# A hybrid decoder layer on one core: key norms and values by transposes, sums and centring on VectorE, and a new written-out order

## The chip, the core and the metric

The kernel runs on one core of a Trainium2 chip, and the times are microseconds on the device. The core has TensorE (PE in the profile, with its weight loads as PEld), VectorE (DVE), ScalarE (ACT), GpSimd (POOL) and SyncE (SP), which here only issues transfers. What counts is the median over several runs of the whole program.

## What is computed

One decoder layer on 512 tokens with 16 meta tokens ahead of them, model width 1024, 16 heads of 64. A first layer norm feeds one projection `h @ w_in`, whose columns are queries, keys and values of a sliding-window attention, the inputs of an RWKV-7 time mixing, and two gates. The two branches are gated and added, then follow an output projection, a layer norm, a squared-ReLU MLP of width 4096 and a last layer norm. The change is in the RWKV branch. Cut to what matters (per head, `N` = 64 channels):

```
kk = kh * k_k
kk = kk / max(sqrt(sum(kk * kk)), 1e-12)                      # the key norm
S  = S * w + (S @ -kk) (kk * a)^T + v k^T                     # 64 x 64 state, per token
y  = S @ r
y  = (y - mean(y)) * rsqrt(mean((y - mean(y))^2) + eps) * lnx_g + lnx_b
y  = (y + sum(r * kh * r_k) * v) * g
```

## The kernel before

**The RWKV branch.** The heads are taken in 8 pairs (`rwkv(j)`, from line 904; two heads fill the 128 partitions), and the 512 tokens in 8 chunks of 64. Channels lie on partitions and tokens along the rows at first. For each pair the projections of key, receptance and value come from `dense` (line 621): the weights are split into a high and a low part, and each product is three matmuls (`three`, line 453, whose lines 454, 455 and 456 are the three). The recurrence is turned into matrix work: scores between the tokens of a chunk (`scores`, 1028), an inverse of each chunk's triangular matrix (its 32 x 32 blocks by substitution on GpSimd, 1119 to 1127; put back together by `inv3` and `inv4` on TensorE, 1143 to 1157), two folding steps (`fold_w`, `fold_g`), and then a chain of 8 links over the chunks: a matmul (`link`, 1243) whose halves are scaled into the next state by VectorE (1225) and ScalarE (1228). `outs` (1248) makes the outputs Y.

**The three places that the change touches.**

- `norms` (984): for each block of 128 tokens one fp32 matmul with the squared keys `sq` as weights and a constant of two columns, `ones2`, as the moving operand. The sums over the 64 channels of each head come out with tokens on partitions, ten columns in all (lines 987 and 988). One more small product (989) writes to the same PSUM tile. VectorE clips (992) and inverts (994) the ten columns, and GpSimd spreads them (999, 1008) to where they scale NT (1039) and others.
- `turn_v` (1093) and `meta0` (1193): the values are turned, so that tokens come to lie on partitions, by fp32 matmuls with a constant `center` = identity minus 1/64 within a head. So the values that enter the recurrence have their mean over the head's channels taken out already, and with them Y: the group norm after it needs no mean.
- the norm of Y (1258 to 1277): ScalarE squares Y out of PSUM (1264), VectorE sums over the 64 channels (1265), scales and adds eps (1266), GpSimd raises to the power -1/2 (1267), VectorE multiplies Y, again out of PSUM, into `yn` (1268), TensorE turns it (1273), ScalarE applies gain and bias (1276). The last pair does this in two halves.

A `pe.transpose` is a matmul with the identity that goes through in one instruction. An fp32 `pe.matmul` shows in the profile as two matmul instructions (x64 for 32 calls).

**What sets the order of the work.** Everything from the first layer norm to the start of the MLP is recorded as operations of a plan (3087 of them; one may issue several instructions), numbered as the program text makes them. The list `ORDER` says in which order they are issued, and `SLOTS` which buffer of its ring each new tile takes: `Plan.order` (354) plays the two lists and asserts that they respect the dependencies. The cost in each `op(...)` is not used by the program. Each engine executes its own operations in that order, and waits where an input is not there. The tiles of PSUM are one ring of 8 banks (`rg`, 491). The MLP behind it (from line 1543) has its own schedule by due times and isn't touched.

Of the kernel before, what the change touches and what calls it, by code (L numbers as in the profile page):

```python
# [14 lines left out]
AF = mybir.ActivationFunctionType  # L15
# [61 lines left out]
for _name, _c in ROWS:  # L77
# [304 lines left out]
def hybrid_layer_kernel(ctx: ExitStack, tc: tile.TileContext, I: dict, out: bass.AP):  # L382
# [26 lines left out]
    def cv(name):  # L409
        a, w = CONSTS[name]  # L410
        return con[:, a : a + w]
# [1621 lines left out]
```

## Time and profile before

| | |
|---|---|
| median of 3 runs | 897.17 us (896.9 to 897.31) |
| the profiled execution, its own time | 897.01 us |
| its span, first to last instruction | 895.2 us |
| mean granted TensorE clock | 0.994 of full speed |
| HBM | 107.56 MB read, 8.21 MB written, 129 GB/s over the span |

Busy times, from the page's first part, are those in which an engine has an instruction in work. The matmuls are pipelined, so that one of 290 ns may start 120 ns after the one before it: what a group of them costs is read from the starts in the timeline. In a view by stretches each row gives a stretch, its length, the busy time and the number of instructions of each engine, the granted clock of TensorE (1.00 is full speed) and the transfers' share. In the waits each row has who waited, for whom, the sum, the count and the longest.

The plan's part ends at about 575 us; the MLP fills the rest.

### The profile page before, as it was taken

What the parts mean: (1) busy time and instruction counts of PE and PEld (TensorE: products, weight loads), DVE (VectorE), ACT (ScalarE), POOL (GpSimd) and SP (SyncE); (2) the same over time, 40 slices, a digit from 0 to 9 for tenths busy, and PEclk for the clock granted to TensorE, in tenths of its full rate; (3) what the DMA queues carried; (4) which work ended last, traced back from release to release, by engine and by line L of the source; (5) the groups of instructions that cost most, each with busy time, mean ns of one, the idle gap of its engine ahead of it and who ended that gap; (6) DMA issues with size and microseconds to landing.
All of it is one profiled execution on the core that took longest, in us unless ns stands there. A gap on an engine that the chain in (4) does not pass through costs nothing.

```text
span 895.2 us, 17524 instructions
## 1 busy us (share of the span) xinstructions
PE 874.7 (98%) x6712; PEld 768.1 (86%) x6712; DVE 674.4 (75%) x1192; ACT 518.8 (58%) x1131; POOL 263.2 (29%) x672
## 2 busy tenths in 40 slices
PE   7999999999999999999989999999999999999996
PEld 6999989888898998887878877988898989888885
DVE  6882976868868678478497689598877896788757
ACT  7854568466575494483663745765556655564710
POOL 3138164183461721822816502000010000000001
PEclk9999999999999999999989999999999999999999
DMA  7443323424143242223243631395687578576322
GB/s 272 127 130 104 86 75 107 117 64 131 55 123 101 78 109 85 84 70 101 72 109 102 197 102 59 97 299 132 178 209 216 141 202 256 133 209 165 98 91 94
DMA packets 73533, 115.87 MB, mean 129 GB/s; under 512 B 40311, under 2 KB 47737, under 8 KB 69481
## 3 DMA queue, kind: packets, MB, share of 16 engines
q1 hardware_dynamic: 69728, 98.89, 35.5%
q0 software_dynamic: 2880, 14.68, 9.0%
q8 instruction: 53, 0.87, 0.4%
q10 hardware_dynamic: 840, 1.17, 0.4%
q14 instruction: 32, 0.25, 0.1%
HBM read 107.56 MB, written 8.21 MB: 129 GB/s over the span
## 4 chain that ended last, share of the span: by engine, by line
PE 90%; DVE 8%; issue 1%; ACT 1%; DMA 1%; POOL 0%; DVEq 0%; SPq 0%; ACTq 0%
PE g L454 12%; PE g L455 11%; PE g L456 11%; PE dnR L1798 7%; PE rq L1704 5%; PE tp L1704 4%; PE dnP L1798 4%; PE last L1798 4%; PE dnT L1798 3%; PE up L454 3%; PE up L455 3%; PE up L456 3%; PE g L1243 2%; PE g L1182 2%; PE g L1297 2%; PE g L1031 1%
## 5 line engine op out<-in xcount | busy, mean ns | idle before, releaser
L454 PE MATMUL g<-hhi,whi 128*128 128x512 f32 (+3 forms) x640 | 213.1, 333 | 0.2 <-DVE GR L1045 0.2
L455 PE MATMUL g<-hlo,whi 128*128 128x512 f32 (+3 forms) x640 | 204.0, 319 | 1.6 <-DVE hlo L817 1.6
L456 PE MATMUL g<-hhi,wlo 128*128 128x512 f32 (+3 forms) x640 | 203.6, 318 | 0.0
L454 PEld LDWEIGHTS g<-hhi,whi 128*128 128x128 f32 x640 | 121.0, 189 | 12.6 <-issue 2.2
L455 PEld LDWEIGHTS g<-hlo,whi 128*128 128x128 f32 x640 | 121.2, 189 | 9.6 <-DVE hlo L817 2.1
L456 PEld LDWEIGHTS g<-hhi,wlo 128*128 128x128 f32 x640 | 120.9, 189 | 8.5 <-DVE wlo L613 0.2
L613 DVE TENSOR_TENSOR wlo<-wraw,whi 128x512 fp32r<-128x512 f32 x126 | 88.3, 708 | 30.4 <-ACT whi L611 29.9
L1122 POOL TENSOR_TENSOR ftmp<-Xf,Nf 108x84 f32<-108x84 f32 (+23 forms) x248 | 86.8, 350 | 74.9 <-DMA Nf<-Nd 45.9
L611 ACT CAST whi<-wraw 128x512 fp32r<-128x512 f32 x126 | 77.0, 619 | 54.0 <-PE g L455 24.6
L1126 POOL TENSOR_TENSOR Xf<-Xf,ftmp 108x84 f32<-108x84 f32 (+23 forms) x248 | 89.6, 361 | 19.0
L1788 POOL DMA_DIRECT2D braw<-in_w_ff_dram x12 | 10.7, 890 | 206.1 <-DVE wlo L1605 87.2
L1228 ACT ACTIVATE Z<-g,PC 64x64 f32<-64x64 f32 x64 | 19.7, 308 | 65.2 <-DVE Z L1225 39.9
L1267 POOL TENSOR_TENSOR rs<-rs,mhalf 128x8 f32<-128x8 f32 (+1 forms) x9 | 14.9, 1659 | 76.2 <-DVE rs L1266 76.2
L1605 DVE TENSOR_TENSOR wlo<-wraw,whi 128x1024 fp32r<-128x1024 f32 x22 | 26.9, 1222 | 13.2 <-ACT whi L1601 10.6
L1225 DVE TENSOR_SCALAR Z<-g,PC 64x64 f32<-64x64 f32 x64 | 17.6, 274 | 23.3 <-PE g L1243 20.8
L1601 ACT CAST whi<-wraw 128x1024 fp32r<-128x1024 f32 x22 | 22.9, 1042 | 17.5 <-PE dnR L1798 8.7
L1605 DVE TENSOR_TENSOR wlo<-braw,whi 128x1024 fp32r<-128x1024 f32 x25 | 30.5, 1219 | 2.4 <-ACT whi L1601 2.4
L1605 DVE TENSOR_TENSOR blo<-braw,bhi 128x1024 fp32r<-128x1024 f32 x25 | 30.5, 1219 | 1.6 <-ACT bhi L1601 1.5
L1601 ACT CAST whi<-braw 128x1024 fp32r<-128x1024 f32 x25 | 26.3, 1053 | 5.4 <-PE rq L1704 4.6
L656 DVE SCALAR_TENSOR_TENSOR res<-g,vc,res 128x256 f32<-128x256 f32 (+2 forms) x34 | 16.2, 481 | 17.0 <-ACT res L653 16.8
L1601 ACT CAST bhi<-braw 128x1024 fp32r<-128x1024 f32 x25 | 26.3, 1051 | 3.4 <-DMA braw<-in_w_ff_dram 3.4
L454 PE MATMUL up<-h1hi,whi 128*128 128x512 f32 x72 | 28.1, 390 | 0.0
(532 smaller groups left out, 2469.6 us busy)
## 6 DMA issues: line engine op xcount, KB each, us to landing
wraw<-in_w_in_dram SPq DMA_DIRECT2D x52, 512.0 KB
braw<-in_w_ff_dram SPq DMA_DIRECT2D x19, 1024.0 KB
wraw<-in_w_ff_dram SPq DMA_DIRECT2D x32, 512.0 KB
braw<-in_w_ff_dram POOLq DMA_DIRECT2D x12, 1024.0 KB, 8.8
wraw<-in_w_out_dram SPq DMA_DIRECT2D x14, 256.0 KB
Nf<-Nd SPq DMA_DIRECT2D x24, 144.0 KB
res<-in_x_dram SPq DMA_DIRECT2D x4, 512.0 KB
G<-in_consts_dram SPq DMA_DIRECT2D x16, 128.0 KB
```

The lines of the kernel that those rows point to most:

```text
L454: pe.matmul(ps, whi, xhi, start=first, stop=False)
L455: pe.matmul(ps, whi, xlo, start=False, stop=False)
L456: pe.matmul(ps, wlo, xhi, start=False, stop=last)
L611: AC(512, lambda hi=hi, qs=qs: act.copy(hi.t, raw.t[:, qs]), plain=True, r=[raw], w=[hi], new=[hi])
L613: f = lambda hi=hi, lo=lo, qs=qs, e=e: e.tensor_tensor(lo.t, raw.t[:, qs], hi.t.bitcast(F32), op=ALU.subtract)
L1122: sub(nj * nt, lambda s=s, nj=nj, nt=nt, tv=tv: pool.tensor_tensor(tv(), Xf.t[:, 0:nj, s : s + 1].to_broadcast([NB, nj, nt]), Nf.t[:, s : ...
L1126: sub(nj * nt, lambda s=s, nj=nj, tv=tv: pool.tensor_tensor(Xf.t[:, 0:nj, s + 1 :], Xf.t[:, 0:nj, s + 1 :], tv(), op=ALU.add), port=1, r=[ ...
L1228: op("ACT", 335, lambda: act.activation(Z.t[H2[1], c, 1, :], src(1), AF.Copy, scale=PC.t[H2[1], last : last + 1]), r=[ps, PC], w=[(Z, ("s" ...
L1601: act.copy(like(s["r"][0][:, :n], s["x"]), s["x"])
L1605: dve.tensor_tensor(lo, s["x"], hi.bitcast(F32), op=ALU.subtract)
L1704: pe.matmul(o, l[:, ks], r[:, k], start=start and k == c == 0, stop=stop and k == 3 and c == 2, skip_group_check=True)
L1798: pe.matmul(acc[b], l[:, as_], r[:, ws], start=first and i == 0 and q == 0, stop=last and i == NP - 1 and q == 2, skip_group_check=True)
```

## The change

It does four things. (1) `norms` turns the squared keys by transposes into a PSUM tile of its own (`kt_`; the first 128 tokens once more into `mt`, for the meta tokens), and VectorE sums each row's 64 channels into `d1`. (2) `turn_v` and `meta0` turn the values by transposes, without centring. (3) So Y has a mean: VectorE sums it over the channels into a new small tile `ym`, and subtracts it (`yn` = Y - mean); the square and the last multiplication take `yn` from SBUF in place of Y from PSUM. (4) The constants `center` and `ones2` (130 columns) go, and `ORDER` and `SLOTS` are replaced by others, over 3105 operations. The words given with the change say that the order was searched with shared PSUM tiles, transfer semaphores and the clock counted.

```diff
-    out["center"] = np.eye(P) - bones / HD
-    out["ones2"] = (p[:, None] // HD) == np.arange(2)[None, :]
...
+    rym = ring("ym", rb, [P, 8], 2)
...
-        mt, d1, dv, dvm = Buf(rg), Buf(rd1), new("dv", rdv), Buf(rdvm)
+        mt, kt_, d1, dv, dvm = Buf(rg), Buf(rg), Buf(rd1), new("dv", rdv), Buf(rdvm)
...
-                pe.matmul(mt.t[:, 2 * i : 2 * i + 2], sq.t[:, t0 : t0 + P], cv("ones2"), start=True, stop=True)
-            pe.matmul(mt.t[:, 8:10], sq.t[:, 0:P], cv("ones2"), start=True, stop=True)
+                pe.transpose(kt_.t[:, i * P : (i + 1) * P], sq.t[:, t0 : t0 + P], ident)
+            pe.transpose(mt.t[:, P : 2 * P], sq.t[:, 0:P], ident)
             pe.matmul(mt.t[0:48, 32:64], BKm.t, AXm.t.rearrange("p e t -> p (e t)"), start=True, stop=True)
 
-        op("PE", 1300, norms, r=[sq, BKm, AXm], w=[(mt, "s")], new=[mt], mode="F")
-        op("DVE", 80, lambda: dve.tensor_scalar(d1.t, mt.t[:, 0:10], 1e-24, None, op0=ALU.max), r=[(mt, "s")], w=[d1], new=[d1])
-
-        op("DVE", 120, lambda: dve.reciprocal(d1.t, d1.t), r=[d1], w=[d1])
+        op("PE", 760, norms, r=[sq, BKm, AXm], w=[(mt, "s"), kt_], new=[mt, kt_], mode="F")
+        DV(512, lambda: dve.tensor_reduce(d1.t[:, 0:8], kt_.t.rearrange("p (u i) -> p u i", i=HD), axis=AX.X, op=ALU.add), r=[kt_], w=[d1], new=[d1])
+
+        def inverse():
+            dve.tensor_reduce(d1.t[:, 8:10], mt.t[:, P : 2 * P].rearrange("p (u i) -> p u i", i=HD), axis=AX.X, op=ALU.add)
+            dve.tensor_scalar(d1.t, d1.t, 1e-24, None, op0=ALU.max)
+            dve.reciprocal(d1.t, d1.t)
+
+        op("DVE", 400, inverse, r=[(mt, "s"), d1], w=[d1])
...
-                pe.matmul(vt.t[:, i * P : (i + 1) * P], v.t[:, t0 : t0 + P], cv("center"), start=True, stop=True)
+                pe.transpose(vt.t[:, i * P : (i + 1) * P], v.t[:, t0 : t0 + P], ident)
...
-            pe.matmul(ms.t[:, 0:P], v.t[:, 0:P], cv("center"), start=True, stop=True)
+            pe.transpose(ms.t[:, 0:P], v.t[:, 0:P], ident)
...
-            AC(n, lambda cs=cs: act.activation(ysq.t[:, cs], Y.t[:, cs], AF.Square), r=[(Y, k) for k in yk(j, h)], w=[(ysq, h)], new=[ysq] if one else [])
+            DV(n, lambda us=us, u8=u8: dve.tensor_reduce(ym.t[:, us], u8(Y.t), axis=AX.X, op=ALU.add), r=[(Y, k) for k in yk(j, h)], w=[(ym, h)], new=[ym] if one else [])
+            DV(n, lambda us=us, u8=u8: dve.scalar_tensor_tensor(u8(yn.t), B64(ym.t[:, us], HD), -1.0 / HD, u8(Y.t), op0=ALU.mult, op1=ALU.add),
+               r=[(ym, h)] + [(Y, k) for k in yk(j, h)], w=[(yn, h)], new=[yn] if one else [])
+            AC(n, lambda cs=cs: act.activation(ysq.t[:, cs], yn.t[:, cs], AF.Square), r=[(yn, h)], w=[(ysq, h)], new=[ysq] if one else [])
...
-            DV(n, lambda us=us, u8=u8: dve.tensor_tensor(u8(yn.t), u8(Y.t), B64(rs.t[:, us], HD), op=ALU.mult),
-               r=[(rs, h)] + [(Y, k) for k in yk(j, h)], w=[(yn, h)], new=[yn] if one else [])
+            DV(n, lambda us=us, u8=u8: dve.tensor_tensor(u8(yn.t), u8(yn.t), B64(rs.t[:, us], HD), op=ALU.mult),
+               port=1, r=[(rs, h)], w=[(yn, h)])
```

The lists `ORDER` and `SLOTS` are left out of this diff. To compare the two orders, the new numbers are matched to the old: the operations keep their program order, two are added in each part of the norm of Y (pairs 0 to 6 have one part, pair 7 two), and in `norms` three operations stand where three stood. 3087 + 2 x 9 = 3105.

More of the change, by code (lines that the diff above doesn't have):

```diff
@@ L1095, in turn_v @@
                 t0 = NMETA + i * P
-                pe.matmul(vt.t[:, i * P : (i + 1) * P], v.t[:, t0 : t0 + P], cv("center"), start=True, stop=True)
-        op("PE", 896, turn_v, r=[v], w=[vt], new=[vt, Z], mode="F")
+                pe.transpose(vt.t[:, i * P : (i + 1) * P], v.t[:, t0 : t0 + P], ident)
+        op("PE", 442, turn_v, r=[v], w=[vt], new=[vt, Z], mode="T")
         for q in range(2):
@@ L1194, in meta0 @@
             pe.transpose(ms.t[0:48, 320:448], BKm.t, ident)
-            pe.matmul(ms.t[:, 0:P], v.t[:, 0:P], cv("center"), start=True, stop=True)
-        op("PE", 335, meta0, r=[BKm, v, XTm, AKm], w=[(ms, 0), (ms, "b")], new=[ms, BTm, SVm, RHm], mode="F")
+            pe.transpose(ms.t[:, 0:P], v.t[:, 0:P], ident)
+        op("PE", 225, meta0, r=[BKm, v, XTm, AKm], w=[(ms, 0), (ms, "b")], new=[ms, BTm, SVm, RHm], mode="F")
         DV(128, lambda: dve.tensor_tensor(BTm.t, ms.t[0:48, 320:448].rearrange("p (h j) -> p h j", h=2), B64(dvm.t, HD), op=ALU.mult),
@@ L1257, in rwkv @@
                w=[(Y, h)], new=[Y] if h == 0 else [], mode="C")
-        ysq, yn, rs = Buf(re_), Buf(re_), Buf(rrs)
+        ysq, yn, rs, ym = Buf(re_), Buf(re_), Buf(rrs), Buf(rym)
         yt, z = Buf(rg), new("z", rz)
```

323 rows, old and new, of tables (ORDER, SLOTS) are left out of this document.

## The prediction, made before the change was run

> **What bounds the kernel now.** I read the page's busy times first, then the chain that ended last, then the busy times by stretches, and last the waits.
>
> ```profile
> span 895.2 us, 17524 instructions
> PE 874.7 (98%) x6712; PEld 768.1 (86%) x6712; DVE 674.4 (75%) x1192; ACT 518.8 (58%) x1131; POOL 263.2 (29%) x672
> ...
> PE 90%; DVE 8%; issue 1%; ACT 1%; DMA 1%; POOL 0%; DVEq 0%; SPq 0%; ACTq 0%
> ```
>
> TensorE has work in flight for 98% of the span, and 90% of the chain that ended last lies on it. The stretches say whether that holds everywhere (columns: stretch, length, busy PE, PEld, DVE, ACT, POOL with instruction counts, granted clock, transfers):
>
> ```profile
> 40.00:400.00 360.00, 359.47 (x3321) 321.53 (x3321) 263.34 (x560) 220.55 (x579) 165.34 (x464) 1.00 0.35 97
> 400.00:440.00 40.00, 37.38 (x363) 31.57 (x362) 29.80 (x64) 22.21 (x62) 18.02 (x39) 1.00 0.32 95
> 440.00:474.00 34.00, 31.34 (x319) 27.23 (x317) 25.47 (x54) 18.03 (x42) 11.18 (x38) 0.90 0.36 97
> 474.00:520.00 46.00, 46.00 (x287) 38.73 (x285) 33.30 (x63) 26.00 (x66) 26.88 (x64) 1.00 0.53 147
> 520.00:575.00 55.00, 54.09 (x468) 45.12 (x467) 45.34 (x93) 33.08 (x79) 6.83 (x8) 1.00 0.28 82
> 575.00:895.20 320.20, 312.68 (x1706) 272.52 (x1704) 248.16 (x301) 167.32 (x236) 21.79 (x24) 0.99 0.60 171
> ```
>
> From 40 to 400 us TensorE is without work for 0.5 us of 360, while VectorE has work for 73%: there the span is TensorE's work, and each us taken off it comes off the time. From 400 to 474 us it lacks 5.3 us, and in the row from 440 us the clock is down to 0.90. The MLP from 575 us on isn't touched: any change has to show before it.
>
> **Term 1, work taken off TensorE.** The chain view merges neighbouring steps of one line, so its lengths are what a group adds to the path, not the pipelined 270 ns of one instruction:
>
> ```profile
> 104.46 0.89 PE g L1096 x8
> ...
> 58.44 0.88 PE g L1069 x8
> ...
> 44.97 0.79 PE g L987 x8
> 45.76 0.22 PE g L988 x2
> 45.98 0.20 PE g L989 x2
> ...
> 46.51 0.12 PE g L455
> ...
> 521.16 0.22 PE g L1195 x2
> ```
>
> L1096 is `turn_v`: four fp32 matmuls, eight instructions, 0.89 us. L1069 is a transpose of the same tile size, one instruction each: eight in 0.88 us. An instruction costs 0.11 us either way, and the transpose needs half as many. So `turn_v` goes from 0.89 to 0.44 (-0.45). `norms` has ten instructions in 0.79 + 0.22 = 1.01 us; five transposes at 0.11 are 0.55 (-0.46; the moving side grows from 2 columns to 128, but these ten already cost 0.10 each, so the two columns saved next to nothing). L989 stays. (L455, a projection's matmul of 266 columns, gives the price of a segment of six: 0.7 us.) `meta0` goes from 0.22 to 0.11 (-0.11). A pair saves 1.02 us, eight pairs 8.2 us. It is worth less only where TensorE then waits for something else, which the next terms hold; it could be 8.5 if `norms` lost exactly half, 0.50 a pair.
>
> **Term 2, work put on VectorE.** No row has these very instructions; the nearest, by group of one shape (mean in ns after the bar):
>
> ```profile
> L1265 DVE TENSOR_REDUCE rs<-e 128x8 f32<-128x512 f32 x4 | 2.7, 686 | 3.7 <-ACT e L1264 3.7
> L1265 DVE TENSOR_REDUCE rs<-e 128x4 f32<-128x256 f32 x2 | 0.8, 420 | 0.2 <-ACT e L1264 0.2
> L1482 DVE SCALAR_TENSOR_TENSOR res<-res,g 128x512 f32<-128x512 f32 x8 | 5.4, 679 | 0.0
> L1198 DVE TENSOR_TENSOR BTm<-g,dvm 48x128 f32<-48x128 f32 x8 | 2.2, 273 | 0.7 <-ACT RHm L1216 0.3 <-ACT SVm L1200 0.2
> ...
> 529.85 2.47 DVE L1186 TENSOR_TENSOR G<-G,g 128x512 f32<-128x512 f32 x4
> ```
>
> A sum over 512 columns takes 0.69 us, the subtraction out of PSUM 0.68 (L1482 reads PSUM too), the small sum over 128 columns about 0.27. Back to back they cost less: four of 0.68 us in 2.47 us are 0.60 from start to start. A pair adds three such and a small one, 3 x 0.60 + 0.27 = 2.1 us, eight pairs 16.6 us, twice what TensorE loses. The square on ScalarE and the last multiplication stay as long as they were. From 40 to 400 us the cover is VectorE's free 27%: with some six pairs' 12.6 us it is busy 276 of then about 354 us, 78%, and TensorE has other projections' matmuls queued. I cost it at nothing there (bounds: 0 and the whole 12.6). A wait is lengthened: VectorE's sum for `d1` stands between `norms` and GpSimd's spreading, so the scaling of NT, the substitution and `inv3` come 0.60 + 0.27 = 0.9 us later. Behind the waiting sum on VectorE are the weights' low parts (L613), which the projections need. The norm of Y gets 1.2 us longer; its result goes through `merge` to the output projection, and where pair 6's does, the row from 474 to 520 us has TensorE busy for 46.00 of 46.00 us: nothing.
>
> Where VectorE has no room is the end of the plan (a stretch, and a row of the timeline):
>
> ```profile
> 550.00:560.00 10.00, 9.38 (x56) 7.71 (x55) 9.86 (x22) 8.38 (x22) 1.70 (x3) 1.00 0.00 0
> ...
> 558.09 0.39 PE L455 MATMUL g<-h1lo,whi 128*128 128x256 f32 x1 [0.32 <-DVE h1lo L1514]
> ```
>
> VectorE is 99% busy there, and TensorE waits 0.32 us for its low part of the MLP's input. Pair 7's norm of Y adds two sums and two subtractions on half tiles at up to 0.42, 1.7 us, just ahead. Some of it falls on time that VectorE spent waiting; I take +1.0 (bounds 0 and 1.7).
>
> **Term 3, the new order, where the old one waits.** Two places.
>
> ```profile
> PE g L1243 <- ACT Z L1228: 2.2, 3, 0.8
> PE g L1146 <- DVE U L1153: 1.4, 2, 1.2
> ```
>
> The first is pair 5's chain of links (410 to 416 us). In the old list three links stand in a row with nothing between, and once two; a link then waits for ScalarE to scale the state. In the new list each of pair 5's links but one pair has a projection segment, a `lora` or an attention product between it and the next. I take 1.5 of the 2.2 us off (bounds 0 and 2.2).
>
> The second is pair 6's inverse, where the projections run out:
>
> ```profile
> 454.00:456.00 2.00, 1.62 (x13) 1.22 (x11) 1.99 (x4) 1.93 (x5) 0.00 (x0) 1.00 0.34 74
> 456.00:458.00 2.00, 1.69 (x27) 1.46 (x28) 1.99 (x5) 1.36 (x4) 0.00 (x0) 1.00 0.66 197
> ...
> 462.00:464.00 2.00, 0.79 (x9) 0.35 (x6) 1.91 (x5) 0.25 (x1) 0.00 (x0) 1.00 0.60 238
> 464.00:466.00 2.00, 1.47 (x34) 1.22 (x34) 1.62 (x5) 0.70 (x2) 0.00 (x0) 0.54 0.35 49
> 466.00:468.00 2.00, 1.77 (x35) 1.51 (x35) 1.91 (x4) 1.94 (x5) 0.00 (x0) 0.50 0.64 184
> 468.00:470.00 2.00, 2.00 (x10) 2.00 (x10) 1.91 (x5) 1.49 (x4) 0.00 (x0) 0.50 0.81 282
> 470.00:472.00 2.00, 2.00 (x37) 1.59 (x37) 1.39 (x4) 0.00 (x0) 0.60 (x1) 0.75 0.23 49
> ...
> 466.08 1.06 PE L1151 MATMUL g<-XB,U 32*32 32x32 f32 x32 [0.42 <-ACT U L1155]
> ```
>
> TensorE is without work for 0.38 + 0.31 + 1.21 + 0.53 + 0.23 = 2.7 us, and after the gap the granted clock is about half for 7 us: busy time by the missing share is 1.47 x 0.46 + 1.77 x 0.50 + 2.00 x 0.50 + 2.00 x 0.25 = 3.1 us. The place costs 5.7 us in all. In the old list nothing but `meta3` stands between `inv3` and `inv4`, and no projection between pair 7's scores and `inv3`. In the new one three segments of pair 7's value projection (2.1 us) stand ahead of `inv3`, the gate's product between `inv3` and `inv4`, one segment between `inv4` and `fold_w`. They fill a wait like the last quoted row's (from the timeline), and are longer than it. Against it: VectorE is 81 to 99% busy in these rows, and `d1` adds 0.9 us to it just there. If the gap closes, the clock stays up with it. I take 3.7 of 5.7 us off (bounds 0 and 5.7; below nothing is the first rival).
>
> **The rest.** Any other order may wait in new places; from 40 to 400 us the old one lost 0.5 us, and I add as much (bounds 0 and 3, the size of the sums in the waits). One bank of PSUM more per pair is held from `norms` to the sum, and Y's bank is free before GpSimd's power rather than after it: nothing either way. The constants shrink by 130 columns, 67 KB less to load: nothing.
>
> **The rule that speaks against it.** Full speed of the clock must survive more transposes:
>
> ```profile
> 553.00:555.00 2.00, 2.00 (x14) 1.67 (x13) 1.93 (x5) 1.97 (x6) 0.31 (x1) 1.00 0.00 0
> ...
> 553.47 1.13 PE L1500 MATMUL g<-con,res 128*128 128x128 f32 x8
> ```
>
> Eight transposes in a row (1.13 us with the last one's way through the array) ran here at a clock of 1.00, and the change makes runs of four and five. The Trainium skill ("TensorE: Matmul & The Clock Gate", Part 4: PE-mode transpose) says that transposes do not count as busy for the clock gate, and that full speed does not engage for them. By that rule a run of them would act as a gap, which the quoted rows do not show for eight; the time by the rule is the third rival's, and by the rows the sum stays as it stands.
>
> **The sum.** -8.2 (term 1) + 1.0 (VectorE at the end) - 1.5 (links) - 3.7 (pair 6's inverse) + 0.5 (new waits) = -11.9 us against the profiled execution's own 897.0 us (its span of 895.2 and 1.8 around it), which is 0.2 below the median 897.17: 885.1.
>
> **The rivals.**
>
> 1. *Only the work comes off.* The inverse of pair 6 waits as long as before, because VectorE, not TensorE's queue, is what ends last there, and `d1` adds its 0.9 us; the links gain nothing. -8.2 + 0.9 + 1.0 = -6.3: 890.7. For it speaks VectorE's 1.6 to 2.0 of each 2.0 us in the rows from 454 to 470. Chance 0.22.
> 2. *Slower: VectorE becomes the bound.* All of its 16.6 us shows on TensorE, as waits for low parts (L613) and for NT behind the new sums: +16.6 - 8.2 = +8.4, 905.4. It decides from the point where more than half of the added work (8.2 of 16.6) is not covered. Against it speaks 263 of 360 us in the row from 40 to 400. Chance 0.05.
> 3. *The clock.* If each pair's new transposes brought one such spell of half clock, 8 x 3.1 = 24.8 on top of -11.9: 909.9. Against it the last quoted rows. Chance 0.02.
> 4. *It doesn't do what it says:* the new order gives back in scattered waits what the transposes save, or they cost as much as two passes: within 1.8 us of 897.0. Chance 0.05.
>
> **How the numbers follow.** The forecast has the remaining 0.66. Its own bounds: all gains full and no new wait, -8.5 - 2.2 - 5.7 = -16.4, 880.6; the first rival with new waits at 0.8 ends at 891.5. The range 880.6 to 891.5 leaves out the rivals 2 to 4 (0.12) and little else. A measurement of this kernel can tell about 0.2%, 1.8 us, from no change. Faster by more: 0.66 + 0.22 = 0.88; within: 0.05; slower: 0.07.
>
> **What would show it.** After: matmul instructions for keys and values halve (L987, L988: 80 to 40; L1096: 64 to 32; L1195: 16 to 8), PE's busy time before the MLP falls by 8 us or more, VectorE's total rises by 16 to 19 us, no stretch of half clock near pair 6's inverse, and the waits of L1243 and L1146 are under 1.5 us together. I am wrong if PE's new waits for VectorE exceed 3 us before the MLP, or if the clock falls at a place where it didn't. Either would show in the waits and in the stretches before 575 us.

## The result, and the profile after

The changed kernel takes 908.45 us (median of 4 runs, 905.1 to 910.98) against 897.04 us before: a ratio of 1.0125 (95% interval 1.0091 to 1.0158), 1.2% slower. The forecast was 885.1 us. The profiled execution took 908.29 us, span 906.5, and showed a mean granted clock of 0.985 (before: 0.994).

The page after, span and busy times:

```profile
span 906.5 us, 17358 instructions
PE 871.8 (96%) x6632; PEld 760.2 (84%) x6632; DVE 693.2 (76%) x1226; ACT 517.5 (57%) x1131; POOL 297.1 (33%) x672
```

TensorE has 80 instructions fewer, as forecast, but its busy time is only 2.9 us shorter while the span is 11.3 us longer: it has no work for 34.7 us instead of 20.5. VectorE has 18.8 us more, inside the forecast 16 to 19. The stretches say where (columns as in the prediction: stretch, length, busy PE, PEld, DVE, ACT, POOL, granted clock, transfers):

```profile
40.00:400.00 360.00, 352.79 (x3202) 312.76 (x3201) 279.00 (x585) 221.71 (x578) 191.13 (x464) 0.99 0.34 94
400.00:440.00 40.00, 37.06 (x357) 31.51 (x358) 29.27 (x60) 15.45 (x36) 11.80 (x26) 0.83 0.25 74
440.00:474.00 34.00, 32.89 (x329) 28.30 (x331) 28.57 (x61) 24.16 (x67) 21.39 (x47) 1.00 0.41 107
474.00:520.00 46.00, 41.69 (x296) 34.53 (x287) 29.13 (x57) 22.84 (x61) 30.39 (x69) 0.96 0.45 134
520.00:575.00 55.00, 50.99 (x405) 39.67 (x405) 49.15 (x99) 28.21 (x67) 6.40 (x7) 1.00 0.35 101
```

From 40 to 400 us, where TensorE lacked 0.5 us of work, it now lacks 7.2; from 474 to 520, where it lacked none, 4.3. In the row from 400 us it works at a clock of 0.83, which by its busy time is 37.06 x 0.17 = 6.3 us. The row from 440 us is the one place that became better: 1.00 instead of 0.90. The waits of TensorE after (line waited at, what ended it, us in total, times, longest):

```profile
PE g L688 <- DMA con<-in_consts_dram: 5.6, 1, 5.6
PE g L1036 <- DVE NBm L1055: 4.6, 1, 4.6
PE g L1248 <- DVE Z L1230: 3.0, 1, 3.0
PE g L1151 <- DVE U L1158: 2.3, 2, 1.9
PE g L1426 <- ACT hhi L1419: 1.9, 1, 1.9
PE g L1281 <- DVE res L1276: 1.3, 1, 1.3
...
PE g L1248 <- ACT Z L1233: 0.7, 1, 0.7
```

(L688 waits at the start for the constants, 3.2 us before; L1036 are the next pair's scores, L1248 the links, L1151 `inv3`, L1426 the output projection, L1281 `turn_y`; numbers of lines are 5 to 8 higher than before.) The single waits are long, and behind the start most of them end with VectorE.

**The longest one.** VectorE's timeline in the changed kernel (start, length, instruction, and in brackets the idle time before it and what ended it), TensorE's row, and SyncE's issues:

```profile
274.50 0.28 DVE L1203 TENSOR_TENSOR BTm<-g,dvm 48x128 f32<-48x128 f32 x1
275.95 0.43 DVE L1158 STREAM_TRANSPOSE U<-XB 32x256 f32<-32x256 f32 x1 [1.17 <-DMA XB<-xtd]
280.80 0.43 DVE L1158 STREAM_TRANSPOSE U<-XB 32x256 f32<-32x256 f32 x1 [4.41 <-DMA XB<-xtd]
281.26 0.18 DVE L1055 TENSOR_TENSOR NBm<-g,dvm 16x32 f32<-16x32 f32 x1
```

```profile
281.50 1.87 PE L1036 MATMUL g<-G,BK 64*128 64x128 f32 x14 [4.55 <-DVE NBm L1055]
```

```profile
273.07 0.58 SPq L1139 DMA_DIRECT2D XB<-xtd  x1
273.70 0.62 SPq L1141 DMA_DIRECT2D XTm<-xtd  x1
274.36 0.63 SPq L1292 DMA_DIRECT2D tbd<-tbh  x1
275.37 0.79 SPq L1139 DMA_DIRECT2D XB<-xtd  x1
```

Pair 3's inverse needs two transfers into XB. The second is issued 2.3 us after the first, behind two others, and has landed at 280.80. VectorE reaches its transpose at 276.4 and stands there for 4.41 us. Behind it in the queue waits NBm of pair 4, a small product of 0.18 us that the scores read, and behind that TensorE. Then the clock falls (stretch, length, busy PE, granted clock, transfers):

```profile
278.00:280.00 2.00, 0.00 (x0) 0.67 0.76 210
280.00:282.00 2.00, 0.50 (x4) 0.50 0.56 189
282.00:284.00 2.00, 2.00 (x22) 0.50 0.52 102
284.00:286.00 2.00, 2.00 (x47) 0.62 0.74 234
286.00:288.00 2.00, 2.00 (x58) 1.00 0.14 20
```

Pair 5 meets the same at 401 us: the second transfer was issued at 396.82 behind three others, VectorE waits 2.91 us, `inv3` on TensorE 1.86, and the clock is at 0.50 from 402 to 414 us.

### The profile page after: what moved, and what is told of

Same layout as the page of the kernel before. It is cut to its first block, busy times and chain, and to the rows that moved or that the text cites. A ratio compares the mean times of both kernels' runs of the same rounds, so it can differ in the third digit from the quotient of the medians.

```text
span 906.5 us, 17358 instructions
## 1 busy us (share of the span) xinstructions
PE 871.8 (96%) x6632; PEld 760.2 (84%) x6632; DVE 693.2 (76%) x1226; ACT 517.5 (57%) x1131; POOL 297.1 (33%) x672
## 5 line engine op out<-in xcount | busy, mean ns | idle before, releaser
L453 PE MATMUL g<-hhi,whi 128*128 128x264 f32 (+3 forms) x640 | 211.5, 330 | 1.3 <-DVE res L1388 0.8
L454 PE MATMUL g<-hlo,whi 128*128 128x264 f32 (+3 forms) x640 | 203.9, 319 | 0.4 <-DVE hlo L787 0.4
L455 PE MATMUL g<-hhi,wlo 128*128 128x264 f32 (+3 forms) x640 | 203.4, 318 | 0.0
L1127 POOL TENSOR_TENSOR ftmp<-Xf,Nf 108x84 f32<-108x84 f32 (+23 forms) x248 | 100.4, 405 | 148.1 <-DMA Nf<-Nd 117.1
L453 PEld LDWEIGHTS g<-hhi,whi 128*128 128x128 f32 x640 | 120.7, 189 | 12.9 <-issue 1.4
L455 PEld LDWEIGHTS g<-hhi,wlo 128*128 128x128 f32 x640 | 120.7, 189 | 8.5
L454 PEld LDWEIGHTS g<-hlo,whi 128*128 128x128 f32 x640 | 120.9, 189 | 7.7 <-DVE hlo L787 0.6
L1131 POOL TENSOR_TENSOR Xf<-Xf,ftmp 108x84 f32<-108x84 f32 (+23 forms) x248 | 105.3, 425 | 18.4
L1613 DVE TENSOR_TENSOR wlo<-wraw,whi 128x1024 fp32r<-128x1024 f32 x22 | 26.9, 1222 | 14.2 <-ACT whi L1609 11.3
L1230 DVE TENSOR_SCALAR Z<-g,PC 64x64 f32<-64x64 f32 x64 | 17.5, 274 | 25.8 <-PE g L1248 12.8
L1426 PE MATMUL g<-whi,hhi 128*128 128x512 f32 x64 | 27.1, 424 | 1.9 <-ACT hhi L1419 1.9
```

Of the source, the lines that this page charges most:

```text
L453: pe.matmul(ps, whi, xhi, start=first, stop=False)
L454: pe.matmul(ps, whi, xlo, start=False, stop=False)
L455: pe.matmul(ps, wlo, xhi, start=False, stop=last)
L1127: sub(nj * nt, lambda s=s, nj=nj, nt=nt, tv=tv: pool.tensor_tensor(tv(), Xf.t[:, 0:nj, s : s + 1].to_broadcast([NB, nj, nt]), Nf.t[:, s : ...
L1131: sub(nj * nt, lambda s=s, nj=nj, tv=tv: pool.tensor_tensor(Xf.t[:, 0:nj, s + 1 :], Xf.t[:, 0:nj, s + 1 :], tv(), op=ALU.add), port=1, r=[ ...
L1426: pe.matmul(ps, hhi[:, k, bs], hi, start=first, stop=False)
```

## The experiments

Theory A: the new order is what costs; B: VectorE's added work is; C: the clock falls because of the transposes. The runs:

| run | order | arithmetic | median us | ratio to before, 95% | span, clock of the profiled execution |
|---|---|---|---|---|---|
| before | old | old | 896.3 to 897.4 | 1 | 895.2, 0.994 |
| after | new | new | 908.45 | 1.0125 (1.0091 to 1.0158) | 906.5, 0.985 |
| `old_order` | old | new | 921.26 | 1.0273 (1.0257 to 1.0288) | 920.6, 0.984 |
| `old_order_norms` | old | norms new | 903.72 | 1.0073 (1.0059 to 1.0087) | 902.1, 0.994 |
| `old_order_centre` | old | centring new | 908.42 | 1.0136 (1.0110 to 1.0162) | 911.5, 0.986 |
| `old_ops` | new | old | 900.61 | 1.0054 (1.0032 to 1.0075) | 904.3, 0.990 |
| `xb_two` | new, 2 moves | new | 898.26 | 1.0006 (0.9995 to 1.0016) | 897.3, 0.993 |
| `xb_together` | new, 8 moves | new | 897.90 | 1.0015 (1.0000 to 1.0029) | 894.0, 0.998 |
| `xb_nbm` | and NBm ahead | new | 896.79 | 0.9998 (0.9988 to 1.0008) | 894.6, 0.996 |
| `xb_norms` | as `xb_nbm` | norms new | 897.39 | 1.0005 (0.9996 to 1.0014) | 895.6, 0.996 |
| `old_ops_xb` | as `xb_nbm` | old | 898.52 | 1.0019 (1.0010 to 1.0028) | 896.1, 0.996 |
| `xb_all` | and 4 moves more | new | 894.60 | 0.9965 (0.9953 to 0.9978) | 893.8, 0.994 |
| `old_ops_all` | as `xb_all` | old | 899.88 | 1.0031 (1.0021 to 1.0042) | 897.8, 0.993 |
| `xb_five` | and 1 move more | new | 895.95 | 0.9981 (0.9972 to 0.9990) | 897.2, 0.994 |

The profiled execution lies 3 to 6 us above the median in `old_ops` (906.69), `old_order_centre` (913.25) and `xb_five` (898.97).

### Order and arithmetic apart

`old_order` keeps the new arithmetic and takes the list of before; the new VectorE operations stand where their readers are:

```diff
 ORDER: the list of before, its numbers mapped to the new operations
+    y's sum (L1269), y's centring (L1270)
     the square (L1272)
     ...
```

> The changed kernel's arithmetic in the order of before: each of the 18 new VectorE operations stands right ahead of the square that reads it, the sum over the squared keys where the maximum stood; three of the norms' TensorE steps go 2 to 4 places down the order because no PSUM bank is free earlier. Theory A (the new order is what costs; the arithmetic alone is a gain): the 8.2 us of TensorE work come off and few waits replace them, 888 to 892 us, ratio 0.990 to 0.995, TensorE's waits for VectorE before 575 us stay below 5 us. Theory B (the added 18.8 us of VectorE work, and GpSimd slowed beside it, is what costs, in whatever order): 904 us or more, ratio 1.008 or more. Theory C (more transposes lower the TensorE clock): the clock below 0.99 though TensorE doesn't wait longer, some 905 us.

921.26 us, 24.7 above the 896.57 of before measured with it: that the arithmetic alone is a gain, theory A, falls for this list. The old list is worse for the new arithmetic than the new list is. VectorE's row from 40 to 400 us and its timeline ahead of one wait:

```profile
40.00:400.00 360.00, 346.84 (x3113) 305.26 (x3112) 262.52 (x552) 205.67 (x542) 165.57 (x451) 0.99 0.33 93
```

```profile
281.96 0.69 DVE L613 TENSOR_TENSOR wlo<-wraw,whi 128x512 fp32r<-128x512 f32 x1
282.57 0.68 DVE L992 TENSOR_REDUCE d<-g 128x8 f32<-128x512 f32 x1
283.17 0.28 DVE L995 TENSOR_REDUCE d<-g 128x2 f32<-128x128 f32 x1
...
283.99 0.67 DVE L1367 TENSOR_TENSOR pown<-g,con 128x512 f32<-128x512 f32 x1
284.58 0.67 DVE L1026 TENSOR_TENSOR e<-g,res 128x512 f32<-128x512 f32 x1
```

```profile
285.31 2.59 PE L1036 MATMUL g<-G,BK 64*128 64x128 f32 x32 [2.77 <-DVE e L1026]
```

VectorE is busy for 73% of those 360 us, its share before, and TensorE lacks 13.2 us of work. At 282.57 the two new sums stand in an unbroken row of VectorE's work, and TensorE's scores wait 2.77 us for the end of that row; from the first sum's start to the next instruction the two take 0.9 us. The share of free time was there; it did not lie where the work was put.

`old_ops` is the other corner: the new list without its 18 new operations, on the kernel before.

> The arithmetic of before in the order of the changed kernel: the 18 new VectorE operations are left out of the order, everything else keeps its place (three dense TensorE steps of pair 3 go up to 7 places down for want of a PSUM bank). Theory A: the waits of TensorE near 281, 401, 490 and 522 us stay, and the 8.2 us of TensorE work are back: 905 to 914 us, ratio 1.009 to 1.019. Theory B: VectorE has its old 674 us of work, the waits go, 893 to 899 us, ratio 0.995 to 1.002. Theory C: clock 0.99 or more, the time within 3 us of before.

900.61 us: the new list costs the old arithmetic 4.1 us, more than theory B's 893 to 899 and less than A's 905 to 914. Neither half of the change is a gain alone (+24.7 and +4.1), and together they cost less than their sum: the new list suits the new work better than the old one does, but not enough. The same place in this run, VectorE and TensorE:

```profile
278.04 0.42 DVE L1153 STREAM_TRANSPOSE U<-XB 32x256 f32<-32x256 f32 x1
281.14 0.43 DVE L1153 STREAM_TRANSPOSE U<-XB 32x256 f32<-32x256 f32 x1 [2.68 <-DMA XB<-xtd]
```

```profile
281.84 1.39 PE L1031 MATMUL g<-G,BK 64*128 64x128 f32 x20 [0.54 <-DVE NBm L1050]
```

The second transpose comes at 281.14, with the new arithmetic at 280.80: the transfer sets this moment, not TensorE. With the old arithmetic TensorE arrives at 281.30 and waits 0.54 us; with the new one it arrives at 276.95 and waits 4.55. The 4.35 us are about what the transposes had saved until then (four pairs at the forecast 1.02 are 4.1); they were given back here in one wait, and the half clock behind it came on top.

### Which half of the arithmetic

Both in the old list; in the one the products with `center` stay, in the other those with `ones2`.

> The order of before with the new key norms alone (transposes and two sums on VectorE, one more PSUM bank held meanwhile; three of these TensorE steps go 2 to 4 places down for want of a bank); the centring stays a product on TensorE, and there are no sums or centring of y. Theory B1 (VectorE's added work is the price in proportion to it: the norms bring some 0.6 us a pair of the 2.1): 3 to 8 of the 24.7 us that both parts cost in this order: 898 to 905 us. Theory B2 (it is the place in the chain: the norms stand ahead of dv, NT and the substitution, on which the whole pair hangs): 12 us or more of them, 908 us or more. Theory A (arithmetic alone is a gain, some 3.7 us of TensorE work): 891 to 895 us.

> The order of before with the new centring alone (v and meta rows are transposed uncentred, y's sums and centring are 18 new VectorE operations right ahead of the squares); the norms stay TensorE products. Theory B1 (price in proportion to VectorE's added work, 1.4 us a pair of 2.1): 14 to 21 of the 24.7 us: 910 to 918 us. Theory B2 (the norms' place in the chain is the price): 2 to 10 us, 899 to 907 us. Theory A: 891 to 895 us.

+7.5 and +12.2 us of the 24.7 for both: in the first run within B1's 898 to 905 us, in the second 1.6 us below its 910 to 918. Roughly the price goes with VectorE's work (681.5 and 685.6 us of it, against 674.4 and 694.7), the remaining 5.0 us come only with both; that they come from the two meeting in one queue is not shown. That the norms' place in the chain (B2) is the main price is refuted. In `old_order` and `old_order_norms` three `norms` also stand 2 to 4 places later for want of a PSUM bank; that was not tried by itself, and neither was another place for the new operations in the old list. The prices hold for these places.

### The two positions

`xb_together` changes nothing but SyncE's order: the second XB transfer stands right behind the first in every pair. In pair 3, the list's entries one below the other:

```diff
 1402   XB, first half (L1139)
+1403   XB, second half (L1139)
 1404   XTm (L1141)
 1785   tbd of pair 4 (L1292)
...
-1403   XB, second half (L1139)
```

> The changed kernel with one edit to its order: in each of the 8 pairs the second of the two transfers that fill XB is issued by SyncE right behind the first, ahead of the up to 3 other transfers that stood between them. Theory A, with its mechanism (VectorE's transpose of XB stands 4 to 20 places behind the second transfer and holds up the queue behind it until that lands): the second transfer starts 1 to 2.3 us earlier in pairs 1, 2, 3, 5, 7; TensorE's wait of 4.6 us near 281 us falls to 2 to 3 us, that of 1.9 us near 401 us to under 1, and the half clock behind them gets shorter: 901 to 905 us, ratio 1.004 to 1.009. Theory B: VectorE has as much to do, 906 to 910 us, ratio 1.010 to 1.015.

897.90 us: 10.5 below the changed kernel, more than theory A itself gave it (3.5 to 7.5). `xb_nbm` also puts NBm ahead of the transpose in pairs 1, 3, 4 and 5:

> As the run before it in this call, and in pairs 1, 3, 4 and 5 the small VectorE multiplication that fills the next pair's NBm, on which TensorE's scores hung near 281 us, stands ahead of the transpose of XB. Theory A: the scores start at 277 us and the wait of 4.6 us there is gone, with 1 to 3 us of half clock: 898 to 903 us, ratio 1.001 to 1.007; the wait may come back in part at the next step that needs XB. Theory B: 906 to 910 us, ratio 1.010 to 1.015.

896.79 us, again below A's range; the two intervals overlap, so NBm's place is not shown to matter once the transfer is early. `xb_two` moves the transfer in pairs 3 and 5 alone:

> The changed kernel (908.5 us) with the second XB transfer right behind the first in pairs 3 and 5 alone; the other six pairs stay as in the changed kernel. If the waits of TensorE near 281 and 401 us, with the half clock behind them, are the whole of what the edit in all pairs gave back (897.9 us): 897 to 900 us, clock 0.99 or more. If the other pairs' transfers matter as well, or the gain is spread: 902 to 906 us.

898.26 us: the two positions hold all of the 10 us. SyncE, VectorE and TensorE in `xb_two` at the first of them:

```profile
272.85 1.26 SPq L1139 DMA_DIRECT2D XB<-xtd  x2
```

```profile
275.91 0.43 DVE L1158 STREAM_TRANSPOSE U<-XB 32x256 f32<-32x256 f32 x1 [1.38 <-DMA XB<-xtd]
276.67 0.43 DVE L1158 STREAM_TRANSPOSE U<-XB 32x256 f32<-32x256 f32 x1 [0.33 <-DMA XB<-xtd]
```

```profile
277.37 2.05 PE L1036 MATMUL g<-G,BK 64*128 64x128 f32 x30 [0.69 <-DVE NBm L1055]
```

The second half is issued some 2 us earlier and is used 4.1 us earlier, and TensorE's 4.55 us become 0.69. Some 2 us of the 4.1 are a shorter way from issue to landing (some 3 us instead of 5.4); why was not tried. In the row from 400 to 440 us the clock is 1.00 instead of 0.83. The gain is not clean: at 285 us a new wait comes, for ScalarE's copy into XB, and the clock falls behind it for 6 us.

```profile
287.59 1.98 PE L1171 MATMUL g<-AT,XB 64*64 64x128 f32 x32 [2.42 <-ACT XB L1162]
```

Over the whole span TensorE's time without work falls from 34.7 to 29.7 us. What the clock costs, as the missing share times TensorE's busy time in each stretch of 2 us, falls from 9.7 to 4.5 us. So about half of what the two positions cost was the clock.

Theory C goes with these runs: `xb_together` has every transpose of the change and ran its profiled execution at 0.998, above before's 0.994 (its twelve executions go from 0.988 to 0.998, the middle is 0.994). In the changed kernel the clock fell where TensorE had stood still.

### What the arithmetic is worth in a repaired order

`old_ops_xb` and `xb_norms` take the list of `xb_nbm` with the old arithmetic and with the new norms alone.

> The arithmetic of before in the repaired new order (the order of the run xb_nbm without its 18 new VectorE operations; 896.8 us with them). If the new arithmetic is a gain once its order is repaired (theory A, 8.2 us of TensorE work): 902 to 905 us. If its VectorE work costs what its TensorE work saves (theory B): 894 to 898 us. If it costs more: 893 us or less, and then the new order, repaired, with the old arithmetic beats the kernel before by 0.4% or more.

> The repaired new order with the new norms alone, old centring. If the norms are the part that costs (theory B2): 896 to 900 us, no better than the run beside it. If the centring is (theory B1, by its share of VectorE's work): 892 to 895 us, below both neighbours. Theory A: 3 to 4 us below the run with the old arithmetic in the same order and 3 to 4 above 896.8 us.

898.52 and 897.39 us, beside 896.79 with all of it: the new arithmetic is worth 1.7 us, and the intervals of the two are apart. The run with the norms alone lies between, but its interval reaches into both, so that the halves are not told apart. One row of each page, old arithmetic and new, in the same list and at the same clock of 0.996:

```profile
PE 872.1 (97%) x6712; PEld 764.0 (85%) x6712; DVE 675.9 (75%) x1192; ACT 518.3 (58%) x1131; POOL 289.3 (32%) x672
```

```profile
PE 864.1 (97%) x6632; PEld 753.5 (84%) x6632; DVE 693.6 (78%) x1226; ACT 518.1 (58%) x1131; POOL 296.5 (33%) x672
```

TensorE's work falls by 8.0 us, as forecast (8.2); the time falls by 1.7, the spans by 1.5. The other 6.5 us are waits, for 17.7 us more of VectorE's work. `xb_all` makes four moves that take operations out from behind waiting ones (the third puts ten substitution steps later, behind the power), `old_ops_all` makes them with the old arithmetic:

```diff
-1859, 1861   casts of weights of pair 5 (ACT, L611)
 1409   copy into XB of pair 3 (ACT, L1162)
+1859, 1861
...
+2786   padding of sb, pair 7 (POOL, L1314)
 2631 to 2641   substitution steps (POOL, L1127, L1131)
-2786
...
+2426   power of rs, pair 6 (POOL, L1275)
 2659 to 2669   substitution steps
-2426
...
+2848, 2849   hhi, hlo of pair 5 (L1419, L1420)
 2867   scaling that waits for rows (DVE, L1446)
...
-2848, 2849
```

> The repaired new order (run xb_nbm, 896.8 us) with four more moves, each of which takes an operation out from behind one that waits: in pair 3 ScalarE's copy into XB ahead of two casts of weights that wait for their transfer (2.07 us of TensorE's time near 287 us); in pair 6 GpSimd's power of rs ahead of eleven substitution steps (2.64 us near 496); in pair 7 GpSimd's padding of sb ahead of eleven such steps (2.25 us near 479); pair 5's hhi and hlo ahead of what waits for w_out and rows (1.92 us near 510). If these waits are what hides the 8.2 us of TensorE work: 888 to 892 us, ratio 0.990 to 0.995. If new waits take their place (the engines are full): 894 to 897 us.

> The order of the run xb_all with the arithmetic of before (the 18 new VectorE operations left out). The difference between the two is what the new arithmetic is worth once the waits are repaired: if it is its 8.2 us of TensorE work, this run is 8 us slower than the run beside it, 896 to 900 us against 888 to 892; if VectorE's work still takes most of it back, they lie within 3 us.

894.60 against 899.88 us: in this list the arithmetic is worth 5.3 us, between the 8 and the 3 of the two readings, and `xb_all` beats the kernel before by 0.35% (0.22 to 0.47). The four moves were chosen by the waits of the new arithmetic; the old arithmetic gained nothing by them (898.52 to 899.88, ratios 1.0019 and 1.0031 with intervals that overlap), so the 5.3 us are the price in a list made for the new arithmetic. The four moves were to bring 5 to 9 us and brought 2.2 (3.0 by the ratios to before), the case of new waits: two of the four waits went (near 287 and 479 us), the one near 496 went from 2.64 to 1.4, and a longer one came in the place of the fourth:

```profile
PE g L1426 <- ACT whi L611: 4.2, 1, 4.2
```

```profile
492.17 10.06 SPq L1443 DMA_DIRECT2D res<-in_x_dram  x2
...
503.23 0.42 SPq L606 DMA_DIRECT2D wraw<-in_w_out_dram  x1
```

The output projection's weights are issued at 503.23, behind a load of x that stands about 10 us at the head of SyncE's queue. `xb_five` lets go of what holds that load:

> The order of the run xb_all (894.6 us) with one move more: in pair 6 GpSimd's addition of bv to z, which xb_all put behind the substitution steps that its second move had delayed, stands ahead of fourteen of them, so that z is finished some 5 us earlier, the slot that SyncE's load of x waits for (10 us at the head of its queue near 492 us) comes free, and the load of w_out's weights behind it starts earlier. If the wait of 4.2 us of TensorE near 508 us, with the clock of 0.93 from 470 to 520 us behind it, hangs on that: 887 to 891 us, ratio 0.989 to 0.994. If the weights are late for another reason: 893 to 896 us.

895.95 us, a miss: the weights were issued 2.7 us earlier and TensorE's wait for them fell to 1.0, but the list's next neighbour came late:

```profile
PE g L1426 <- ACT hhi L1419: 4.1, 1, 4.1
```

```profile
513.70 0.63 ACT L1419 ACTIVATE hhi<-e 128x512 fp32r<-128x512 f32 x1 [6.37 <-DMA e<-md]
```

The load of pair 6's merged rows stands on SyncE behind a store that waits for the end of GpSimd's substitution, which now ends at 510.3 us instead of 507.0. Single moves by hand shift the wait from one transfer to the next here; `xb_all` is the best of the versions tried.

## Why the prediction was wrong

It forecast 885.1 us, and gave faster a chance of 0.88; the time was 908.45.

- **Term 1, TensorE's work (-8.2): right.** 8.0 us in the same list at the same clock. The instructions halved as said. Wrong was that "each us taken off it comes off the time": the new arithmetic took 1.7 us off the time in the list of `xb_nbm`, and 5.3 in that of `xb_all`.
- **Term 2, VectorE's work, "I cost it at nothing" from 40 to 400 us: this step failed.** The amount was nearly right (16.6 forecast, 18.8 measured). The cover was read from the share, 73% busy with 27% free. VectorE works its queue in order, and the free time stood in front of instructions that wait, while TensorE hung on the ones behind. In the old list, where little else differs, the new arithmetic cost 24.7 us net of what TensorE saves, more than the whole 20.3 us by which VectorE's work grew there (674.4 to 694.7); the clock, weighted by TensorE's busy time, is 10 of the 24.7 (3.1 us before, 13.1 in the profiled `old_order`). The Trainium skill ("TensorE: Matmul & The Clock Gate", Part 1, "Architectural detail") says that VectorE's queue is strictly first in, first out; the trace agrees, with 0.18 us of NBm held up 4.41 us by the instruction ahead. At the end of the plan, where +1.0 was taken, TensorE's waits for VectorE (L1508 and L454, before L1500 and L455) rose from 0.6 to 1.3 us, near the forecast.
- **Term 3, the two places: right, and more than forecast; the same lines wait elsewhere.** The links of pair 5 wait 0.7 us for ScalarE instead of 2.2 (-1.5 forecast, -1.5 measured). At pair 6's inverse TensorE stops for 0.42 us at 470 us and the clock stays:

```profile
470.00:472.00 2.00, 1.58 (x37) 1.08 (x37) 1.97 (x7) 1.02 (x4) 0.00 (x0) 1.00 0.92 249
472.00:474.00 2.00, 2.00 (x61) 1.81 (x64) 1.96 (x5) 1.46 (x4) 0.00 (x0) 1.00 0.80 207
```

  Some 5.3 of 5.7 us are gone there, 3.7 were forecast. But the sign given for this term, under 1.5 us for the waits of the links and of `inv3` together, did not come: they are 3.0 + 0.7 + 2.3 = 6.0 us after, with 3.0 for VectorE in one link at 490 us and 1.9 at pair 5's `inv3`. The order mended the two places it was read for and opened others.
- **The rest, "+0.5" for new waits (bounds 0 to 3): this step failed by most.** I priced a new order by what the old one lost. From 40 to 575 us TensorE lacks 19.6 us of work instead of 6.7, +12.9. Two positions of one transfer held 10 us of the result. They could have been read from the diff: in the old list VectorE's transpose stands 19 to 37 places behind the second XB transfer, in the new one 10 in pair 3 and 4 in pair 5. The places alone would not have given the price: pairs 1 and 7 have 9 and 6, and VectorE waits there for 0.63 us at most.
- **The clock behind a wait** was priced at pair 6 as a gain and nowhere as a loss. The mean clock of 0.985 instead of 0.994 would be (0.015 x 906.5) - (0.006 x 895.2) = 8.2 us, but it also counts time in which TensorE has no work. Weighted by TensorE's busy time in stretches of 2 us, the loss is 9.7 us after and 3.1 before, +6.6.

The balance: -8.0 of work, +14.2 of time without work (12.9 of it from 40 to 575 us) and +6.6 of clock give +12.8, against 11.3 in the spans; 1.5 us are not accounted for. Of the rivals the first (890.7) had a gain too, and fell with the time. The second had nearly the time (905.4) and half the mechanism: VectorE's work did show on TensorE, but through its order and the transfers in it, not as late low parts. The fourth named scattered waits and gave them 8 us; they were 13, and drew the clock with them. The third fell with `xb_together`. Of its signs to watch, waits on VectorE of over 3 us and a clock that falls in new places, both came.

## What to carry to other kernels

An engine's free share covers added work only where the queue is free; ask what stands ahead of and behind each new instruction, and what the one ahead waits for. Work saved on the bounding engine makes it arrive earlier at the next transfer: before counting a gain, look for the transfer whose landing sets the pace, and for what its issue stands behind. Price a new order from its own list, position by position between an issue and its first user, and add to each wait of some us what the clock may lose behind it.

## What the runs showed of the hardware

- **Most of the scatter between executions of one program goes with the clock.** The changed kernel's own four runs go from 905.1 us at 0.993 to 910.98 at 0.985; `xb_together` from 895.76 at 0.998 to 901.9 at 0.988, some 6 us for 0.01. Not all of it does: `xb_together` also took 897.88 and 901.18 us, both at 0.991.
- **The length of a gap doesn't settle whether the clock falls.** In the changed kernel's gap of 4.55 us it fell to 0.50 some 1.7 us after TensorE's last work, and stayed there until 285.5 us; after 1.86 us near 401 it was at 0.50 for 12 us; after 2.07 us near 285 in `xb_nbm` it stayed at 1.00. Nearest to each other are `xb_two`, with the wait of 2.42 us shown above, and `xb_together`, which waits 2.37 us at the same step (each with the stretch behind it):

```profile
288.00:290.00 2.00, 2.00 (x33) 0.50 0.72 204
```

```profile
287.82 1.10 PE L1171 MATMUL g<-AT,XB 64*64 64x128 f32 x32 [2.37 <-ACT XB L1162]
288.00:290.00 2.00, 2.00 (x37) 1.00 0.80 224
```

  The Trainium skill ("TensorE: Matmul & The Clock Gate", Part 1, "HAM oscillation") puts the limit at gaps over about 3.4 us. The traces don't agree: the clock fell behind gaps of 1.86 and 2.42 us, and 1.7 us into the long one. What else counts is left open.
- **GpSimd's substitution steps are slower in the new order, whatever the arithmetic**: 425 ns the step in the changed kernel, 421 in `old_ops`, 364 in `old_order`, 361 before (the steps of L1131, 248 of each). VectorE's added work is not the reason. The trace shows what the slow steps have in common: beside them VectorE runs instructions whose two inputs both lie in SBUF. In these four traces a step with no more than 0.1 us of such work beside it took on average 0.02 us or less over the shortest of its shape (at most 0.4), a step with more 0.24 to 0.34 us (at most 1.7). The old list sets 46 of the 248 beside such work (51 in `old_order`), the new one 79 (75 in `old_ops`). No run changed this by itself.
